# Output projection of a hybrid attention block: seven block products for the pooled channels, three raw buffers for the pages, halves of the residual loaded behind them

## The chip, the cores and the metric

The kernel runs on one core of one Trainium2 chip. The metric is the device time of one execution in microseconds (us). The kernel before took 1030.73 us, the median of 3 runs (1030.71 to 1030.99). The engines are named as the profile names them: PE (TensorE, the matrix unit), DVE (VectorE), ACT (ScalarE), POOL (GpSimd) and SP (SyncE, which issues most of the DMA transfers). Each engine takes its instructions in the order in which the program wrote them, and an instruction that waits holds up everything behind it on its engine.

## The reference

One block over x (1024 tokens of 1024 channels, float32): attention with forget gates on 8 heads of 64, beside it four groups of 128 channels of causal pooling, one output projection over both, and a gated MLP.

```python
h = rmsnorm(x, norm1_g[layer])
proj = jnp.einsum('bsd,de->bse', h, w_in[layer])
...
attn = forgetting_attention(to_heads(q), to_heads(k), to_heads(v), log_f)
attn = attn.transpose(0, 2, 1, 3).reshape(B, S, ATTN_WIDTH)
pool = multiscale_pool(u, w_pool[layer], pool_scale[layer])
mixed = jnp.concatenate([attn, pool], axis=-1)
x = x + jnp.einsum('bse,ed->bsd', mixed, w_out[layer])
h2 = rmsnorm(x, norm2_g[layer])
gate = jnp.einsum('bsd,df->bsf', h2, w_gate[layer])
up = jnp.einsum('bsd,df->bsf', h2, w_up[layer])
x = x + jnp.einsum('bsf,fd->bsd', jax.nn.silu(gate) * up, w_down[layer])
return rmsnorm(x, final_g)
```

The change is in the line `x = x + mixed @ w_out`: 1024 tokens x 1024 channels times 1024 x 1024.

## The kernel before, in words

**Precision.** A float32 operand is kept as two tiles, a high and a low part (`split`, L119: ACT copies the high part, L120; DVE or POOL subtracts it from the source, L121). One product is three matmuls into the same PSUM bank (`mm3`, L159 to L163: high by high, high by low, low by high). In the profile the page of W_out is h_wo, l_wo (hl_wo where both parts lie in one tile), the page of the mixed channels h_mix, l_mix. A page is 128 channels by 1024 (tokens, or output channels): 512 KB raw, one DMA to a tile r_wo or r_mix, one copy on ACT, one subtraction on DVE or POOL.

**Order.** The program runs first the value and pooling projections, then `project(0)` (queries and keys of a pair of heads), and then `attend(0)` to `attend(3)` (L711), one for each pair of heads. The pool results go to DRAM (mixd, pages 4 to 7) before attend 0 begins. `attend` writes the steps of its eight jobs (a head and a block of 256 queries each) one after the other and takes, behind each step, pieces of a generator `fill`, so many for each job as `counts` says. A job's steps are: scores of the next job (z, two matmuls a bank, L617 and L618), on DVE the masked reduction (p<-z,wmask, L620), on ACT the exponential (L626), on DVE the reciprocal (rr, L628), on POOL the normalisation (p<-p,rr, L629), on PE the transposes of p (tp, L643), their copies th on ACT (L647) and tl on DVE (L648), the value products (po, L657), and at, which goes to mixd. Fill is what PE does in between: in attends 0 to 2 the query, key and value products of the pairs to come (qk, hTh and hTl are the normalised input), in attend 3 the output projection. The tiles s_0 and s_1 hold the queries and keys of a head; they are put together by moves from a tile hi and one lo (L569 to L573), and four augmented rows come from augd (L549), all issued on SP.

**Output projection.** Its eight pages of 128 channels are taken in three parts over all 8 row blocks of 128 tokens (the order is `ORDER`, 0, 4, 1, 5, 2, 3, 6, 7) and both halves of the output channels. `first_rows` (L832; banks o4) takes pages 4 and 5, `second_rows` (L859; banks o6) takes 6, 7 and 0, and `last_row` (L888; banks o2), behind attend 3, takes 1, 2 and 3. Each block is summed in a bank of 128 x 512 (tag "m", two of them) and then added on DVE to x2, which begins as the residual x (L814, L826; x_r and x_s in the profile). x2 lies where hTh and hTl lay: it can be loaded only when the last qk matmul of attend 3's queries and keys has read them. `first_chunk` loads and splits page 4 of both operands and loads page 5 of mix during attend 2. All raw pages share the tag "wr" with two buffers, or take what `first_rows` names. `x2_load` (L797) loads a whole row of x, 512 KB.

**SP's queue** carries the pages, the rows of x, the moves into s and the stores of at, in the order of the program. There are no priorities: a load that waits for its buffer holds up what is written behind it.

**Other names.** vpool's tag "vc" holds pf01 (a pooling tile), later values of a pair of heads, page VC, and last t4l of the MLP, which r_gu_P (its first weights, L1011) precedes. `wmask` is the causal mask, wr a raw page, NPAIR is 4, PAIR is (2, 3, 0, 1).

## Time and profile before

| what | us |
|---|---|
| median of the runs | 1030.73 |
| the profiled execution | 1031.67 |
| its span in the trace | 1029.9 |
| VectorE busy | 780.2 |
| ScalarE busy | 473.2 |
| GpSimd busy | 398.2 |

Busy time by stage, from the windows of the trace:

| from to | what runs | PE | DVE | POOL | DMA share |
|---|---|---|---|---|---|
| 90 to 124 | end of the pooling, start of attend 0 | 34.00 of 34 | 15.79 | 2.94 | 0.48 |
| 124 to 260 | attends 0 to 2 | 136.00 of 136 | 91.78 | 33.87 | 0.36 |
| 264 to 282 | start of attend 3 | 17.33 of 18 | 15.95 | 6.73 | 0.91 |
| 282 to 300 | attend 3 | 18.00 of 18 | 14.63 | 6.90 | 0.59 |
| 300 to 351 | attend 3 to its end | 51.00 of 51 | 34.29 | 21.36 | 0.23 |

The granted clock of TensorE is 1.00 in each of these windows. Busy time of PE is counted from a matmul's start to its modelled end, and matmuls overlap; a gap shorter than that overlap doesn't show in it. Waits are put down to what came last.

### The profile page before, as it was taken

What the parts mean: (1) busy time and instruction counts of PE and PEld (TensorE: products, weight loads), DVE (VectorE), ACT (ScalarE), POOL (GpSimd) and SP (SyncE); (2) the same over time, 40 slices, a digit from 0 to 9 for tenths busy, and PEclk for the clock granted to TensorE, in tenths of its full rate; (3) what the DMA queues carried; (4) which work ended last, traced back from release to release, by engine and by line L of the source; (5) the groups of instructions that cost most, each with busy time, mean ns of one, the idle gap of its engine ahead of it and who ended that gap; (6) DMA issues with size and microseconds to landing.
All of it is one profiled execution on the core that took longest, in us unless ns stands there. A gap on an engine that the chain in (4) does not pass through costs nothing.

```text
span 1029.9 us, 15123 instructions
## 1 busy us (share of the span) xinstructions
PE 1020.5 (99%) x5428; PEld 878.3 (85%) x5428; DVE 780.2 (76%) x1232; ACT 473.2 (46%) x759; POOL 398.2 (39%) x317
## 2 busy tenths in 40 slices
PE   9999999999999999999999999999999999999997
PEld 8988888998888888888888888888888888888886
DVE  7565566776786579887978767676777999888887
ACT  7434355665665257544443343343443443333346
POOL 4350121214336043366656646647546610000045
PEclk9999999999999999999999999999999999999999
DMA  7214434333643134333222423333336774353424
GB/s 252 53 46 143 106 81 103 83 95 95 220 176 110 47 118 133 93 113 92 93 82 93 133 83 104 121 104 111 103 121 227 282 251 165 134 187 96 154 93 164
DMA packets 108795, 130.28 MB, mean 126 GB/s; under 512 B 8040, under 2 KB 71024, under 8 KB 108720
## 3 DMA queue, kind: packets, MB, share of 16 engines
q1 hardware_dynamic: 97216, 108.18, 33.5%
q10 hardware_dynamic: 10784, 19.16, 4.9%
q0 software_dynamic: 720, 1.97, 0.5%
q8 instruction: 43, 0.70, 0.3%
q14 instruction: 32, 0.26, 0.1%
HBM read 86.29 MB, written 33.03 MB: 116 GB/s over the span
## 4 chain that ended last, share of the span: by engine, by line
PE 95%; DVE 2%; DMA 1%; issue 1%; ACT 1%; POOL 0%; ACTq 0%; POOLq 0%; DVEq 0%
PE gu_P L162 10%; PE gu_P L161 10%; PE gu_P L163 10%; PE d L161 6%; PE d L163 6%; PE d L162 6%; PE po L657 3%; PE tp L643 3%; PE qk L161 3%; PE qk L162 3%; PE qk L163 3%; PE o L162 3%; PE o L163 3%; PE o L161 3%; PE v L374 2%; PE z L618 2%
## 5 line engine op out<-in xcount | busy, mean ns | idle before, releaser
L162 PE MATMUL d<-d,d 128*128 128x512 f32 (+1 forms) x308 | 118.7, 388 | 0.0
L163 PE MATMUL d<-d,d 128*128 128x512 f32 (+1 forms) x308 | 118.0, 388 | 0.0
L629 POOL TENSOR_SCALAR p<-p,rr 128x128 f32<-128x128 f32 (+3 forms) x64 | 48.8, 769 | 177.1 <-DVE rr L628 135.8
L161 PE MATMUL d<-d,d 128*128 128x512 f32 x308 | 108.0, 388 | 0.0
L120 ACT ACTIVATE d<-r_f 128x1536 fp32r<-128x1536 f32 (+1 forms) x28 | 38.7, 1384 | 107.5 <-PE d L162 103.1
L1579 POOL TENSOR_SCALAR sse<-sse 128x1 f32<-128x1 f32 x7 | 3.5, 494 | 167.6 <-ACT junk L1575 167.6
L162 PEld LDWEIGHTS d<-d,d 128*128 128x128 f32 x308 | 57.8, 188 | 12.1 <-DVE d L121 0.2
L163 PEld LDWEIGHTS d<-d,d 128*128 128x128 f32 x308 | 57.8, 188 | 11.9
L161 PEld LDWEIGHTS d<-d,d 128*128 128x128 f32 x308 | 57.8, 188 | 11.9
L120 ACT ACTIVATE gu_P_h<-s 128x1024 fp32r<-128x1024 f32 (+1 forms) x38 | 36.4, 967 | 61.9 <-PE gu_P L162 31.1
L626 ACT ACTIVATE p<-p,mn 128x128 f32<-128x128 f32 (+3 forms) x64 | 49.4, 773 | 32.0 <-DVE mn L620 29.0
L121 DVE TENSOR_TENSOR gu_P_l<-s,gu_P_h 128x1024 fp32r<-128x1024 f32 (+1 forms) x38 | 54.9, 1454 | 6.6 <-ACT gu_P_h L120 6.4
L648 DVE TENSOR_TENSOR tl<-tp,th 128x512 fp32r<-128x512 f32 (+1 forms) x80 | 49.5, 633 | 9.6 <-ACT th L647 8.5
L121 DVE TENSOR_TENSOR d<-r_f,d 128x1536 fp32r<-128x1536 f32 (+1 forms) x28 | 45.8, 1636 | 6.6 <-ACT d L120 6.5
L163 PE MATMUL qk<-hTh,l_qk 128*128 128x512 f32 x128 | 50.7, 396 | 0.0
L161 PE MATMUL qk<-hTh,h_qk 128*128 128x512 f32 x128 | 50.6, 395 | 0.0
L162 PE MATMUL qk<-hTl,h_qk 128*128 128x512 f32 x128 | 50.4, 394 | 0.0
L1684 DVE TENSOR_TENSOR x2f_s<-d,x2f_s 128x512 f32<-128x512 f32 x64 | 42.4, 683 | 9.9 <-PE d L163 9.9
L647 ACT ACTIVATE th<-tp 128x512 fp32r<-128x512 f32 (+1 forms) x80 | 42.5, 551 | 16.2 <-PE tp L643 13.2
L1161 ACT ACTIVATE sn_sU<-gu_P 128x512 f32<-128x512 f32 x44 | 26.2, 595 | 47.7 <-PE gu_P L163 33.1
L620 DVE CUSTOM_DVE_ANT_0 p<-z,wmask 128x128 f32<-128x128 f32 (+3 forms) x64 | 33.7, 535 | 13.6 <-PE z L618 9.7
L643 PE MATMUL tp<-ident,p 128*128 128x128 f32 x288 | 43.2, 274 | 0.0
(1180 smaller groups left out, 3376.6 us busy)
## 6 DMA issues: line engine op xcount, KB each, us to landing
r_f<-hsdP SPq DMA_DIRECT2D x77, 256.0 KB
r<-in_w_gate_dram SPq DMA_DIRECT2D x44, 256.0 KB
r<-in_w_up_dram SPq DMA_DIRECT2D x44, 256.0 KB
r_wd<-in_w_down_dram SPq DMA_DIRECT2D x22, 512.0 KB
hsdP<-f ACTq DMA_DIRECT2D x40, 256.0 KB
s<-hi SPq DMA_DIRECT2D x64, 128.0 KB
hsdP<-h ACTq DMA_DIRECT2D x23, 256.0 KB
x<-in_x_dram SPq DMA_DIRECT2D x8, 512.0 KB
```

The lines of the kernel that those rows point to most:

```text
L120: mark["hi"] = nc.scalar.activation(out=hi, in_=src, func=AF.Copy)
L121: return eng.tensor_tensor(out=lo, in0=src, in1=f32(hi), op=ALU.subtract)
L161: nc.tensor.matmul(ps, lh, rh, start=start, stop=False, **kw)
L162: nc.tensor.matmul(ps, lh, rl, start=False, stop=False, **kw)
L163: mark["mm"] = nc.tensor.matmul(ps, ll, rh, start=False, stop=stop, **kw)
L620: nc.vector.tensor_tensor_reduce(out=pr[:, n0:n1], in0=z, in1=wmask[:, S - n + n0 : S - n + n1], scale=1.0, scalar=mn, op0=ALU.add, op1=AL ...
L626: nc.scalar.activation(out=pr[:, :n], in_=pr[:, :n], func=AF.Exp, scale=-1.0, bias=mn, accum_out=rs)
L629: nc.gpsimd.tensor_scalar(out=pr[:, :n], in0=pr[:, :n], scalar1=rr, scalar2=1.0, op0=ALU.mult, op1=ALU.mult)
L643: nc.tensor.transpose(tp[:, w : w + P], probs[h, 2 * sb + a][:, s * P : (s + 1) * P], ident)
L647: nc.scalar.activation(out=th[:, :w], in_=tp[:, :w], func=AF.Copy)
L648: nc.vector.tensor_tensor(out=tl[:, :w], in0=tp[:, :w], in1=f32(th[:, :w]), op=ALU.subtract)
L1684: added = nc.vector.tensor_tensor(out=row, in0=ps, in1=row, op=ALU.add)
```

## The change

The pooled channels are pages 4 to 7, 512 of the 1024 in the sum. Tokens are cut into two halves of 512, channels 512 to 1023 into two halves of 256 and output channels into two halves of 512, so that this part is a product of 2 x 2 blocks. Before it took 8 block products; now it takes 7 (P1 to P7), whose operands are blocks or sums of blocks of mix and of W_out. Each block product is 24 matmuls of 128 x 512: four row blocks of 128 tokens, for each two pages of 128 channels, three matmuls each. Page 0 is added to the same banks with `whole`, in part as products of their own (`alone`), and pages 1, 2 and 3 stay in the last rows.

The sums of blocks are formed in attends 0 and 1 by `side_steps`, a second generator: four rounds, two for W_out and two for mix. A round loads four half rows of 128 x 512 quarters (1 MB) into vpool's "vc", makes four sums of 128 x 512 on POOL and stores 1 MB to DRAM (sumd). The pages of P1 to P7 are loaded from mixd, W_out or sumd in halves of 256 KB. Raw pages have two buffers "wr" and a third, "or"; the pages of the last rows ("LATE") come in halves into "hi". A product's bank is read by DVE, added to x2, while the bank stays open and the next product of the chain is added to it. Rows of x are loaded as halves, from the fifth step on behind the page that was issued last.

```diff
+    def quarter_load(r):
+        kind, i = rounds[r]
+        t = quarters[r] = vpool.tile([P, 4, 512], F32, tag="vc", bufs=1, name=f"quarters{r}")
+        for k in range(2):
+            dst = t[:, 2 * k : 2 * k + 2, :].rearrange("p a e -> p (a e)")
+            nc.sync.dma_start(out=dst, in_=page_source(kind, NPAIR + 2 * k + i))
+    def quarter_sums(r):
...
+        for out, in0, in1, op in todo:
+            nc.gpsimd.tensor_tensor(out=out, in0=in0, in1=in1, op=op)
+            yield
+            yield
+    def side_steps():
+        for r in range(len(rounds)):
+            quarter_load(r)
+            for _ in range(3):
+                yield
+            yield from quarter_sums(r)
+            for _ in range(2):
+                yield
+            quarter_store(r)
+            yield
...
-    attend(0, project(1), [5, 4, 4, 3, 8, 6, 6, 0])
-    attend(1, both(project(2), project_v23()), [10, 7, 6, 8, 10, 8, 12, 0])
+    side = side_steps()
+    attend(0, project(1), [5, 4, 4, 3, 8, 6, 6, 0], side=side)
+    attend(1, both(project(2), project_v23(side)), [10, 7, 6, 8, 10, 8, 12, 0], side=side)
...
-    fill = both(first_rows(), second_rows())
+    fill = output_steps()
...
+    def part(ps, k, c, start, stop):
+        (ah, al), (bh, bl) = operands["mix", k], operands["wo", k]
+        for i in range(2):
+            ts, hs = slice(i * 512 + c * P, i * 512 + (c + 1) * P), slice(i * 512, (i + 1) * 512)
+            mm3(ps, ah[:, ts], al[:, ts], bh[:, hs], bl[:, hs], start and i == 0, stop and i == 1, True)
...
+    SPLITS = [
+        ("mix", "P2", M, G, -1), ("wo", "P2", O, V, 0), ("mix", "P7", M, G, 2), ("wo", "P7", O, V, 3),
+        ("mix", "P4", ST1, G, 5), ("wo", "P4", VC, V, 6), ("mix", "P1", M, G, 8), ("wo", "P1", O, V, 9),
+        ("mix", "P6", M, G, 12), ("wo", "P6", O, G, 13), ("mix", "P5", ST0, G, 14), ("wo", "P5", W, V, 15),
+        ("mix", "P3", ST1, G, 16), ("wo", "P3", VC, G, 18), ("wo", 1, O, V, 24), ("mix", 1, M, G, 24),
+        ("wo", 2, O, V, 26), ("mix", 2, M, G, 27), ("wo", 3, W, V, 30),
+    ]
+    HALF_LOADS = {
+        0: [(0, 0), (1, 0)], 1: [(2, 0), (3, 0)], 5: [(4, 0), (5, 0)], 7: [(6, 0), (7, 0)],
+        12: [(0, 1), (1, 1)], 16: [(2, 1), (3, 1)],
+    }
...
+        def alone(c):
+            for tt in (NH + 2 * c, NH + 2 * c + 1):
+                ps = fresh("o0", tt)
+                whole(ps, tt, 1, True, True)
+                add_to(tt, 1, ps)
+        def link(k, down, right, start, stop, more=False):
+            def do(c):
+                ps = fresh(f"o{k}", c) if start else held[c]
+                part(ps, k, c, start, stop and not more)
+                tt = c + down * NH
+                if more:
+                    whole(ps, tt, right, False, stop)
+                add_to(tt, right, ps)
...
+        order = [(alone, 0), (alone, 1)]
+        order += chain(("P2", 0, 0, True, True, True))
+        order += chain(("P7", 1, 1, True, False), ("P4", 1, 0, False, True, True))
+        order += chain(
+            ("P1", 0, 0, True, False), ("P6", 1, 0, False, False), ("P5", 1, 1, False, False),
+            ("P3", 0, 1, False, True, True),
+        )
...
-    attend(3, fill, [3, 3, 4, 4, 4, 4, 3, 2], drain=False)
+    attend(3, fill, [2, 3, 4, 3, 4, 4, 3, 2], drain=False)
```

The list of PE's instructions has 5404 matmuls and transposes after the change, 5428 before. Three places of the lists follow.

POOL at the start of attend 0, behind the four stores to augd. Before, the normalisations of the first head's blocks (p_0, p_1, ...) are next:

```order
L629 TENSOR_SCALAR p_0_1205<-p_0_1205,rr_0_1213 128x128
L629 TENSOR_SCALAR p_1_1216<-p_1_1216,rr_1_1224 128x256
L629 TENSOR_SCALAR p_2_1258<-p_2_1258,rr_2_1266 128x384
L629 TENSOR_SCALAR p_3_1272<-p_3_1272,rr_3_1280 128x512
L629 TENSOR_SCALAR p_4_1310<-p_4_1310,rr_4_1323 128x640
```

Now, at the same place (quarters_1240 is round 1's tile, quarters_1479 round 2's, in the same memory):

```order
L770 TENSOR_TENSOR quarters_1240<-quarters_1240 128x512 x4
L770 TENSOR_TENSOR quarters_1479<-quarters_1479 128x512 x3
L631 TENSOR_SCALAR p_0_1209<-p_0_1209,rr_0_1217 128x128
L631 TENSOR_SCALAR p_1_1220<-p_1_1220,rr_1_1228 128x256
L631 TENSOR_SCALAR p_2_1265<-p_2_1265,rr_2_1273 128x384
L770 TENSOR_TENSOR quarters_1479<-quarters_1479 128x512
L631 TENSOR_SCALAR p_3_1279<-p_3_1279,rr_3_1287 128x512
```

Seven sums, and with them one round's store and the next round's load, have come between the augd stores and the first normalisation.

SP at the start of attend 3 (r_wo, r_mix are pages, x_r and x_s rows of x, s the operands of the scores). Before:

```order
L754 DMA r_wo_3529<-in_w_out_dram 128x1024
L798 DMA x_r_3491<-in_x_dram 128x1024
L569 DMA s_1_3_0_3168<-hi_3_1_3301 64x512
L570 DMA s_1_3_0_3168<-hi_3_1_3301 64x512
L573 DMA s_1_3_0_3170<-lo_3_3167 64x512
L798 DMA x_r_3491<-in_x_dram 128x1024
L754 DMA r_wo_3541<-in_w_out_dram 128x1024
```

Now (r_mixP_3549 is the raw page of P7's mix, r_woP_3546 that of P2's W_out):

```order
L822 DMA r_mixP_3549<-sumd_mix_1205 128x512
L822 DMA r_mixP_3549<-sumd_mix_1206 128x512
L569 DMA s_1_3_0_3205<-hi_3_1_3338 64x512
L570 DMA s_1_3_0_3205<-hi_3_1_3338 64x512
L573 DMA s_1_3_0_3207<-lo_3_3204 64x512
L891 DMA x_r_3528<-in_x_dram 128x512
L891 DMA x_r_3529<-in_x_dram 128x512
L891 DMA x_s_3531<-in_x_dram 128x512
L822 DMA r_woP_3546<-in_w_out_dram 128x512 x2
```

The first row of x has moved behind the moves into s, as halves of several rows, and the first page of W_out behind three of them.

DVE at the start of attend 3, from the first add into x2 to the low part of P2's W_out page (o_4 to o_7 are the banks of `alone`). Before, the page's low part (l_wo, page 5) stands ahead of the first add, as the first of these rows:

```order
L121 TENSOR_TENSOR l_wo_3537<-r_wo_3529,h_wo_3536 128x1024
L648 TENSOR_TENSOR tl_3_3_3110<-tp_3_3_3105,th_3_3_3109 128x384
L648 TENSOR_TENSOR tl_0_0_3137<-tp_0_0_3132,th_0_0_3136 128x384
L620 ISA p_7_3373,mn_7_0_3377<-z_7_0_3374,wmask 128x512
L620 ISA mn_7_0_3377 128x1
L628 RECIPROCAL rr_6_3357<-rs_6_3355 128x1
L826 TENSOR_TENSOR x_r_3491<-o_0_0_3550,x_r_3491 128x512
```

Now, the last twelve of the eighteen rows that begin with the add of o_4:

```order
L670 TENSOR_TENSOR at_3_3160<-po_3_3070,at_3_3160 64x256
L622 ISA p_7_3410,mn_7_512_3419<-z_7_512_3416,wmask,mn_7_0_3414 128x512
L622 ISA mn_7_512_3419 128x1
L622 ISA p_0_3456,mn_0_0_3460<-z_0_0_3457,wmask 128x128
L622 ISA mn_0_0_3460 128x1
L895 TENSOR_TENSOR x_s_3531<-o_6_3623,x_s_3531 128x512
L650 TENSOR_TENSOR tl_1_0_3295<-tp_1_0_3289,th_1_0_3294 128x512
L622 ISA p_1_3480,mn_1_0_3484<-z_1_0_3481,wmask 128x256
L622 ISA mn_1_0_3484 128x1
L650 TENSOR_TENSOR tl_1_1_3325<-tp_1_1_3320,th_1_1_3324 128x384
L895 TENSOR_TENSOR x_s_3533<-o_7_3628,x_s_3533 128x512
L121 TENSOR_TENSOR l_woP_3584<-r_woP_3546,h_woP_3583 128x1024
```

The page's low part now stands behind four adds, each of which needs its half row of x.

More of the change, by code (lines that the diff above doesn't have):

```diff
@@ L578, in project, with project_v23 @@
                 yield
-    def project_v23():
+    def project_v23(side):
+        for _ in side:
+            pass
         vtile(2)
@@ L709, in tile_kernel, with attend @@
     begun = set()
-    def attend(p, fill, counts, drain=True):
+    def attend(p, fill, counts, drain=True, side=iter(())):
         if p == 0:
@@ L742, in both, with page_source @@
             yield from g
-    attend(0, project(1), [5, 4, 4, 3, 8, 6, 6, 0])
-    attend(1, both(project(2), project_v23()), [10, 7, 6, 8, 10, 8, 12, 0])
+    def page_source(kind, c):
+        row = (PAIR[c] if c < NPAIR else c) * P
+        return mixd[c] if kind == "mix" else w_out[0, row : row + P, :]
+    sumd = {(kind, i): dram.tile([P, 4, 512], F32, name=f"sumd_{kind}{i}") for kind in ("mix", "wo") for i in range(2)}
+    rounds = [("wo", 0), ("wo", 1), ("mix", 0), ("mix", 1)]
+    quarters = {}
@@ new lines, in tile_kernel, with ahead_of @@
+    FIRST_LATE = len(SPLITS) - len(LATE)
+    THIRD.update(entry[:2] for entry in SPLITS[2:FIRST_LATE:3])
+    HALF_LOADS = {
+        0: [(0, 0), (1, 0)], 1: [(2, 0), (3, 0)], 5: [(4, 0), (5, 0)], 7: [(6, 0), (7, 0)],
+        12: [(0, 1), (1, 1)], 16: [(2, 1), (3, 1)],
+    }
+    def ahead_of(s):
+        for n, (kind, c, to, eng, at) in enumerate(SPLITS):
+            if at == s:
+                split_page(kind, c, to, eng)
+                after = n + 1 if (kind, c) in LATE else n + 3
+                if after < len(SPLITS) and (SPLITS[after][:2] not in LATE or (kind, c) in LATE or after == FIRST_LATE):
+                    raw_page(*SPLITS[after][:2])
+        for tt, hf in HALF_LOADS.get(s, []):
+            with tc.issue_after(loads["page"].ins) if s >= 5 else ExitStack():
+                half_load(tt, hf)
@@ L871, in page @@
+    raw_page(*SPLITS[1][:2])
+    raw_page(*SPLITS[2][:2])
+    for tt in range(NH, NT):
+        half_load(tt, 1)
+    ahead_of(-1)
+    fill = output_steps()
+    attend(3, fill, [2, 3, 4, 3, 4, 4, 3, 2], drain=False)
+    last = {
+        k: [operands[kind, 1]] for k, kind in (("lhs", "mix"), ("rhs", "wo"))
+    }
     def page(tag, name):
```

127 lines of the change are left out of this document (72 added, 55 removed).

## The prediction

> **What bounds the kernel now.** I read the page's busy times first, then the chain that ended last, then TensorE's waits, and only then the timeline.
>
> ```profile
> PE 1020.5 (99%) x5428; PEld 878.3 (85%) x5428; DVE 780.2 (76%) x1232; ACT 473.2 (46%) x759; POOL 398.2 (39%) x317
> PE 95%; DVE 2%; DMA 1%; issue 1%; ACT 1%; POOL 0%; ACTq 0%; POOLq 0%; DVEq 0%
> PE o L161 <- ACT h_wo L120: 0.4, 1, 0.4
> PE o L162 <- DVE l_wo L121: 0.2, 1, 0.2
> ```
>
> TensorE (PE) is busy 99% of the span, 95% of the chain lies on it, and in the output projection it waits twice, for one page. So a matmul that goes away is worth its place in PE's queue, and everything else is worth only what it makes PE wait. The price of a matmul is not the mean that the groups give (first row; then the timeline, start and duration):
>
> ```profile
> L162 PE MATMUL o<-l_wo,h_mix 128*128 128x512 f32 x64 | 25.1, 392 | 0.2 <-DVE l_wo L121 0.2
> ...
> 274.22 0.39 PE L163 MATMUL o<-h_wo,hl_mix 128*128 128x512 f32 x1
> 274.44 0.39 PE L161 MATMUL o<-h_wo,h_mix 128*128 128x512 f32 x1
> 274.67 0.39 PE L162 MATMUL o<-l_wo,h_mix 128*128 128x512 f32 x1
> 274.90 0.39 PE L163 MATMUL o<-h_wo,l_mix 128*128 128x512 f32 x1
> ```
>
> One lasts 0.39 us from start to end, but the next starts after 0.22 or 0.23 us: three spacings make 0.68 us, so I price it at 0.2275 us. The 392 ns counts the overlap twice.
>
> **What goes.** Channels 512 to 1023 of the product took 8 blocks x 24 matmuls; now they take 7 x 24. So 24 matmuls go, which is the whole difference in PE's row count: 24 x 0.2275 = 5.46 us (by 392 ns it would be 9.4). The adds of banks into x2 stay 32. The two waits above go as well, because after wo0 the first products now need no second page:
>
> ```profile
> 269.34 0.39 PE L618 MATMUL z<-s,s 68*128 68x512 f32 x1
> 270.16 0.73 PE L161 MATMUL o<-h_wo,h_mix 128*128 128x512 f32 x2 [0.43 <-ACT h_wo L120]
> 270.90 0.27 PE L618 MATMUL z<-s,s 68*128 68x128 f32 x1
> 271.42 0.50 PE L162 MATMUL o<-l_wo,h_mix 128*128 128x512 f32 x1 [0.24 <-DVE l_wo L121]
> ```
>
> The matmul at 269.34 would be followed at 269.57, but the next starts at 270.16, 0.59 late; the narrow one at 270.90 takes about 0.06 and the next is 0.46 late. Together 1.05 us.
>
> **What comes: the sums in attend 0.** VectorE (DVE) reads pf01 last at 93.58 + 1.23 = 94.81, and its space takes the first quarters; SP reaches that load behind the augd rows, at 95.27 + 0.76 = 96.0. The rows are from the timeline (start, duration), a group (busy, mean ns) and the rates of the DMA view.
>
> ```profile
> 93.58 1.23 DVE L121 TENSOR_TENSOR pl<-pf,ph 128x1024 fp32r<-128x1024 f32 x1
> 95.27 0.76 SPq L549 DMA_DIRECT2D s<-augd  x2
> 115.32 1.50 POOL L629 TENSOR_SCALAR p<-p,rr 128x128 f32<-128x128 f32 x3 [38.94 <-DVE rr L628]
> 119.45 0.27 PE L643 MATMUL tp<-ident,p 128*128 128x128 f32 x1
> L121 POOL TENSOR_TENSOR l_u<-r_u,h_u 128x1024 fp32r<-128x1024 f32 x4 | 10.5, 2628 | 10.7 <-ACT h_u L120 10.7
> 350.93 0.33 SPq L880 DMA_DIRECT2D r_mix<-mixd  x1
> 353.44 0.63 ACT L120 ACTIVATE mix_h<-r_mix 128x512 fp32r<-128x512 f32 x1 [2.13 <-DMA r_mix<-mixd]
> GB/s 0 0 0 0 173 15 0 129 70 269 398 386 386 339 293 222 369 345 351 234 234 164 269 316 328 398 316 316 386 398 398 410 445 433 386 386 445 410 375 375
> ```
>
> The last row is the rate from 262 to 276 us, when transfers queue; I take 350 GB/s. A lone 256 KB took 2.51 us to its reader, so about 1.75 beside its bytes. One megabyte is then 1.75 + 3.0 = 4.75 us. A sum over 128x512 is half an l_u: 1.31. The line: load lands 101.3 (0.55 more for the mixd stores beside it), four sums to 106.5, store out by 112.0 (0.75 for the key moves beside it), next load by 117.1, three sums to 121.0. Only then does POOL reach p_0, p_1, p_2, which take 1.5: done at 122.5. Before, POOL was free from 76 us, and p_0 lay ready 3.6 us ahead of its transpose at 119.45. In the new order PE's transpose of p_0 falls 1.36 us later (six more matmuls of 0.2275 ahead of it), that of p_2 at about 121.6. So PE waits 0.9; I take **1.0**, bounds 0 (no neighbours in the queues) and 3.5 (both round trips lose 1.3 to the moves). The later rounds stand ahead of normalisations that are 4 us or more early, and I cost them at nothing; without that cover each is worth up to one sum, 1.3.
>
> The Trainium skill (DMA: Bandwidth & Descriptors, Anatomy of one DMA) has about 2.0 us fixed and 436 GB/s for a transfer from GpSimd's queue, hence an estimate of 4.4 us for a megabyte, and this wait would shrink to nothing and the total to 1027.1. The 5.42 us for half a megabyte below speaks against such a rate in a crowded queue.
>
> **What comes: the entry of attend 3.** The first x rows now arrive as halves behind pages, and four adds follow single products. Below, a row of the chain that ended last, then the timeline and the groups of 260 to 351 us.
>
> ```profile
> 263.61 5.42 DMA r_wo<-in_w_out_dram
> 263.64 0.33 PE L617 MATMUL z<-s,s 128*128 128x384 f32 x1
> 264.51 0.48 SPq L569 DMA_DIRECT2D s<-hi  x1
> 266.33 1.54 SPq L798 DMA_DIRECT2D x_r<-in_x_dram  x1
> L814 DVE TENSOR_TENSOR x_r<-o,x_r 128x512 f32<-128x512 f32 x14 | 9.5, 683 | 4.6 <-PE o L163 4.5
> L648 DVE TENSOR_TENSOR tl<-tp,th 128x512 fp32r<-128x512 f32 x20 | 13.5, 686 | 2.8 <-ACT th L647 2.6
> L648 DVE TENSOR_TENSOR tl<-tp,th 128x384 fp32r<-128x384 f32 x13 | 7.1, 551 | 0.3
> L620 DVE CUSTOM_DVE_ANT_0 p<-z,wmask 128x512 f32<-128x512 f32 x5 | 3.4, 682 | 0.6 <-PE z L618 0.6
> L668 DVE TENSOR_TENSOR at<-po,at 64x256 f32<-64x256 f32 x13 | 5.5, 420 | 4.4 <-ACT at L667 4.3
> 270.14 1.23 DVE L121 TENSOR_TENSOR l_wo<-r_wo,h_wo 128x1024 fp32r<-128x1024 f32 x1 [1.31 <-ACT h_wo L120]
> ```
>
> PE's rows from the first z behind the last qk product (263.64) to the first that reads the low part of woP2: 14 matmuls of 0.2275, 22 z (3.87), 21 transposes (2.34), 20 value products (2.14), together 11.5 us, so it is wanted at 275.2. On SP the halves stand behind three s moves, where a row went out at 266.33; with 1.75 and a quarter to three quarters of a megabyte at 350 the first lands at about 269.2. DVE is in order: behind the first add stand three more adds, tl of 128x384, 128x512 and 128x384, two reductions of z 7, the small ones of z_0 and z_1, at, and then l_woP2. By starts (each about 0.07 before the end of the one ahead): 2.5 + 1.6 + 2.1 + 0.5 + 1.2 = 7.9, done at 277.1. PE waits **1.9**. Bounds: 0.9 (half lands a microsecond earlier) and 4.5 (it lands as late after its issue as the page in the chain's row, 5.42 us). Queued behind are the reductions and tl of the next heads, which hold z banks; that is in the upper bound.
>
> **What comes: behind it.** Two more groups of DVE from 260 to 351 us carry this part.
>
> ```profile
> L620 DVE CUSTOM_DVE_ANT_0 p<-z,wmask 128x384 f32<-128x384 f32 x5 | 2.7, 548 | 0.4 <-PE z L618 0.4
> L121 DVE TENSOR_TENSOR hl_wo<-r_wo,hl_wo 128x1024 fp32r<-128x1024 f32 x1 | 1.2, 1216 | 0.0
> ```
>
> hl_woP4 (low part) stands on DVE directly behind the reduction of z_2 and is wanted 1.7 us after that z's last matmul; 0.55 + 1.22 + 0.1 is 1.9: **0.3** with ACT's part, bounds 0 and 2. Banks are now read open: P1, P6, P5, P3 share one, and the next product may not write before DVE has added it. At two places only the other bank's six matmuls lie between, 6 x 0.2275 = 1.36 us; an add takes 0.68, which leaves as much for the hand-over. That hides unless the wo1 and wo2 splits (1.22 + 2 x 0.69 = 2.6) stand ahead of the add, as they do once: **0.3**, bounds 0 and 1.0. Last, r_gu_P's first DMA waits for PE's last use of woP3 and stands on SP ahead of wo3's second half:
>
> ```profile
> 354.16 0.69 DVE L121 TENSOR_TENSOR mix_l<-r_mix,mix_h 128x512 fp32r<-128x512 f32 x1 [0.41 <-ACT mix_h L120]
> 264.00:282.00 18.00, 17.33 (x101) 15.02 (x101) 15.95 (x41) 13.40 (x27) 6.73 (x5) 1.00 0.91 300
> ```
>
> A half took from 350.93 to 354.85, 3.9 us, to be split; with 0.45 for the row ahead 4.4. Its low part is wanted 4.3 us after that use: **0.4** with the gate's bytes beside it, bounds 0 and 1.2. The extra splits (ten rows on ACT, five on DVE) run where DVE is 15.95 of 18 us busy, which is why I trust no cover at the entry. From the last rows on, all five queues have the same rows in the same order, so what PE has won there it keeps.
>
> **Sum.** Profiled execution 1031.67 (span 1029.9 and 1.77 around it): - 5.46 - 1.05 + 1.0 + 1.9 + 0.3 + 0.3 + 0.4 = 1029.06. It was 0.94 above the median of the runs, 1030.73, so 1028.1 there.
>
> **Rivals.** (1) All covers hold: the stalls come to 0 to 2 us, the time to 1024.2 to 1026.2. For it: the bound of zero is real for four of five terms. Against: DVE's load at the entry. (2) The entry's burst lands late and every later DVE row with it: stalls of 5.5 to 8.6, 1029.7 to 1032.8, no change that can be told. For it: DMA is 0.91 busy from 264 to 282. (3) Slower: POOL's line in attend 0 takes over. If the megabyte legs run at the rate at which the key moves go (about 200 GB/s, next row), each is 7.0 us, sums end at 126.2, p_2 at 127.7, 6.1 us after PE wants it; sums at 1.87 (what such an operation takes on POOL when DVE reads beside it) add 3.9. With 2.9 from the other terms: 1033.2 to 1037.1.
>
> ```profile
> GB/s 351 337 2 19 117 201 201 117 0 239 361 0 152 215 199 33 325 274 0 152 213 199 101 0 0 0 155 215 199 31 0 0 75 213 192 119 0 0 0 0
> L1197 POOL TENSOR_TENSOR f<-sn_sP,sn_sU 128x512 f32<-128x512 f32 x8 | 15.0, 1870 | 0.0
> ```
>
> That row is 90 to 125 us: 200 in the moves, gaps between them, which a megabyte over all partitions may fill. It turns slower than before when the three legs take more than 18.5 us together; I have 15.8.
>
> **The numbers.** Forecast (stalls 2 to 5.5: 1026.2 to 1029.7) 0.45; rival 1 0.22; rival 2 0.18; rival 3 0.15. A measurement of this kernel tells about 0.2%, 2.06 us, from no change: faster is below 1028.67, slower above 1032.79. Faster: 0.22 and two thirds of the forecast's, 0.52; same: the rest of it and nearly all of rival 2, 0.32; slower: 0.16. The range leaves out a tenth at each end: 1024.6 to 1033.4.
>
> **What would show it.** 5404 matmuls and transposes on PE; a PE gap at the transposes of p_0 to p_2 near 121 us whose releaser is POOL; a gap before the first product with l_woP2 with DVE's adds ahead of it; no wait for h_wo at 269. I am wrong if PE waits somewhere not named here, above all for a normalisation behind rounds 2 to 4, or if the two traces drift apart after 410 us.

## The result, and the profile after

The changed kernel takes 1039.46 us (median of 4 runs, 1037.67 to 1040.88), the kernel before beside it 1030.86 (1030.71 to 1031.46): ratio 1.0081, 95% interval 1.0064 to 1.0099. It is slower by 8.6 us. 1028.1 was forecast, and the time lies above the range. The profiled execution of the changed kernel takes 1039.72 us, 8.05 more than the profiled one of before (1031.67).

The page of the changed kernel, busy times and the engines of the chain that ended last:

```profile
PE 1022.0 (98%) x5404; PEld 875.5 (84%) x5404; DVE 784.0 (76%) x1237; ACT 479.0 (46%) x768; POOL 425.2 (41%) x337
PE 89%; DMA 3%; DVE 3%; issue 1%; ACT 1%; POOL 1%; SPq 0%; ACTq 0%; POOLq 0%; DVEq 0%
```

The 24 matmuls are gone (5404 against 5428), yet PE is busy longer, 1022.0 against 1020.5 us: the same matmuls last longer somewhere. And the chain has left PE: 95% of it lay there, now 89%, with DMA and DVE at 3% each.

PE's waits over the changed kernel's whole span (what waits, what released it: us in total, times, longest):

```profile
PE o L161 <- ACT h_wo L120: 2.0, 2, 1.7
PE oP L161 <- ACT h_woP L120: 1.8, 1, 1.8
...
PE qk L161 <- ACT p L628: 0.9, 1, 0.9
PE tp L645 <- DVE tl L650: 0.8, 1, 0.8
PE po L659 <- DVE tl L650: 0.5, 1, 0.5
```

These make 6 us, less than half of the 13.5 (8.05, and the 5.46 of the matmuls) that have to be found. The windows show where PE had less to do; the columns are length, then busy time and instructions of PE, PEld, DVE, ACT and POOL, PE's granted clock, DMA share and GB/s. Before:

```profile
282.00:300.00 18.00, 18.00 (x115) 16.10 (x114) 14.63 (x40) 9.59 (x18) 6.90 (x8) 1.00 0.59 220
300.00:318.00 18.00, 18.00 (x108) 15.75 (x107) 14.83 (x38) 13.96 (x28) 11.37 (x10) 1.00 0.38 120
351.00:375.00 24.00, 24.00 (x116) 20.02 (x114) 12.89 (x19) 8.37 (x14) 4.18 (x7) 1.00 0.32 112
```

After:

```profile
264.00:282.00 18.00, 16.18 (x90) 13.23 (x89) 13.83 (x38) 12.26 (x24) 7.36 (x5) 0.95 0.73 213
282.00:300.00 18.00, 17.75 (x97) 15.37 (x95) 11.71 (x28) 10.26 (x19) 9.69 (x9) 0.96 0.82 272
300.00:318.00 18.00, 16.34 (x90) 13.34 (x91) 14.48 (x39) 10.40 (x23) 6.51 (x7) 1.00 0.45 139
351.00:375.00 24.00, 21.45 (x99) 16.67 (x98) 15.15 (x23) 10.81 (x18) 8.12 (x6) 1.00 0.39 122
```

PE is short of work at three places of attend 3: the entry (264 to 282), the middle (300 to 318) and the end (351 to 375). In the first two rows its clock is 0.95 and 0.96 where it was 1.00; that is where the matmuls grew longer.

To add the losses up I gave each row of PE, in order, the spacing it has when nothing disturbs it (0.2275 us for 128x512, as in the prediction, and so for the narrower ones) and subtracted the running sum from the start times. What that difference grows by in a stage was lost there, by waits or by the clock. Minus the same of before, each from one profiled execution, in us (good to about half a microsecond, since a loss at a border can fall to either side); the last column is the time until 420 us at half clock, of which at most half is lost:

```
                           to 262   262-290   290-312   312-374   sum   at half
changed kernel               2.1       3.5       3.7       3.9    13.2       3.4
before, 24 matmuls less      0.0       0.2      -0.1       1.5     1.6       0.0
changed, no sums             0.0       3.9       4.3       4.7    12.9       3.4
changed, wo3 raw apart       1.4       4.3       1.0       4.7    11.4       3.4
changed, five buffers        2.0       5.2       4.7       4.6    16.5      10.2
changed, sums contiguous     1.4       2.7       7.3       5.1    16.5      13.7
changed, x rows whole        2.9       4.5       3.3       4.1    14.8       3.4
changed, all rows whole      3.2       3.4       0.8       6.0    13.4       6.8
changed, woP2 first          1.5       3.8       3.6       3.7    12.6       3.4
changed, 9 more at entry     2.3       0.3       7.2       3.4    13.2       6.8
changed, 18 more at end      2.5       4.6       3.2       0.7    11.0       3.4
five buffers, x ahead        2.4       3.7       0.8       3.5    10.4       3.4
no x rows                    1.4       0.9       3.5       4.7    10.5       3.4
five buffers, no x rows      1.3       0.1       2.3       2.7     6.4       0.0
before, loads in halves     -0.1       4.2       0.8       0.2     5.1       3.4
```

For the changed kernel 13.2 - 5.46 = 7.7 of the 8.05 us. The rows below it are the experiments; matmuls that they add count as work and not as lost.

Entry, after, from the timeline: SP issues woP2's load, ACT makes its high part, PE reads it.

```profile
270.89 0.86 SPq L822 DMA_DIRECT2D r_woP<-in_w_out_dram  x2
277.60 1.06 ACT L120 ACTIVATE h_woP<-r_woP 128x1024 fp32r<-128x1024 f32 x1 [2.53 <-DMA r_woP<-in_w_out_dram]
278.71 0.51 PE L161 MATMUL oP<-h_woP,h_mixP 128*128 128x512 f32 x1 [1.77 <-ACT h_woP L120]
281.91 0.63 PE L161 MATMUL oP<-h_woP,h_mixP 128*128 128x512 f32 x1
282.33 0.63 PE L162 MATMUL oP<-l_woP,h_mixP 128*128 128x512 f32 x1
283.84 0.39 PE L163 MATMUL oP<-h_wo,hl_mix 128*128 128x512 f32 x1
```

The page takes 6.7 us from its issue to its first reader. PE waits 1.77 us, and then matmuls start 0.42 us apart, not 0.2275. Two-microsecond windows show why:

```profile
278.00:280.00 2.00, 1.29 (x9) 1.21 (x10) 0.99 (x2) 2.00 (x5) 0.00 (x0) 1.00 0.58 153
280.00:282.00 2.00, 2.00 (x8) 1.31 (x7) 2.00 (x7) 1.95 (x7) 0.00 (x0) 0.55 0.85 260
282.00:284.00 2.00, 2.00 (x7) 1.58 (x6) 1.91 (x6) 1.47 (x5) 1.84 (x3) 0.60 0.85 264
284.00:286.00 2.00, 2.00 (x11) 1.62 (x10) 0.86 (x4) 0.00 (x0) 1.36 (x3) 1.00 0.71 221
```

Behind the wait the clock is at half: a mean of 0.55 over 2 us is 1.8 us at half, 0.60 is 1.6. These 3.4 us do the work of 1.7, so 1.7 us more are lost. DVE's adds, which the prediction had ahead of the page's low part, come second:

```profile
279.01 0.69 DVE L895 TENSOR_TENSOR x_s<-o,x_s 128x512 f32<-128x512 f32 x1 [1.08 <-DMA x_s<-in_x_dram]
279.62 1.22 DVE L121 TENSOR_TENSOR l_woP<-r_woP,h_woP 128x1024 fp32r<-128x1024 f32 x1
```

The low part is done at 280.84, and the first product that reads it starts at 280.89, about 0.3 us later than it could at half clock.

Middle, after: the chain that ended last, 292 to 307 us.

```profile
290.04 2.42 POOL l_mixP L121
...
292.85 4.24 DMA r_woP<-in_w_out_dram
...
297.18 1.07 ACT h_woP L120
...
298.27 1.24 DVE l_woP L121
...
299.52 0.32 SPq L822
...
299.89 3.77 DMA r_mixP<-sumd_mix
...
303.74 0.04 ACT h_mixP L120
...
304.70 0.48 ACT th L649
...
305.21 0.04 DVE tl L650
```

No matmul stands in it. A page's low part on POOL frees a raw buffer, the next page goes into it, ACT makes its high part, DVE its low part, that frees the buffer, and the next page is issued. From one load (292.46) to the next (299.52) it is 7.0 us, with three buffers 2.3 us a page. And ACT is in order: th, the high half of the transposed weights of attention, waits behind h_mixP, tl behind th, PE behind tl. Which page's high part stands ahead of th is a matter of ACT's order; in this execution it is h_mixP, which waits 1.93 us for its page, and hl_woP, whose load went out earlier (297.49) and for which ACT doesn't wait, comes after it:

```profile
303.74 1.06 ACT L120 ACTIVATE h_mixP<-r_mixP 128x1024 fp32r<-128x1024 f32 x1 [1.93 <-DMA r_mixP<-sumd_mix]
306.62 1.06 ACT L120 ACTIVATE hl_woP<-r_woP 128x1024 fp32r<-128x1024 f32 x1
```

End, after, timeline:

```profile
361.47 0.33 SPq L996 DMA_DIRECT2D r_mix<-mixd  x1
362.65 0.33 SPq L822 DMA_DIRECT2D r_wo<-in_w_out_dram  x1
366.05 0.63 ACT L120 ACTIVATE h_wo<-r_wo 128x512 fp32r<-128x512 f32 x1 [1.45 <-DMA r_wo<-in_w_out_dram]
366.73 0.50 PE L161 MATMUL o<-h_wo,mix_h 128*128 128x512 f32 x1 [1.72 <-ACT h_wo L120]
```

wo3's halves are issued behind the last splits, and PE has come to them before they land.

### The profile page after: what moved, and what is told of

Read it like the earlier page. It is cut to its first block, busy times and chain, and to the rows that moved or that the text cites. A ratio compares the mean times of both kernels' runs of the same rounds, so it can differ in the third digit from the quotient of the medians.

```text
span 1037.9 us, 15214 instructions
## 1 busy us (share of the span) xinstructions
PE 1022.0 (98%) x5404; PEld 875.5 (84%) x5404; DVE 784.0 (76%) x1237; ACT 479.0 (46%) x768; POOL 425.2 (41%) x337
## 4 chain that ended last, share of the span: by engine, by line
PE 89%; DMA 3%; DVE 3%; issue 1%; ACT 1%; POOL 1%; SPq 0%; ACTq 0%; POOLq 0%; DVEq 0%
PE gu_P L162 10%; PE gu_P L161 10%; PE gu_P L163 10%; PE d L162 6%; PE d L161 6%; PE d L163 6%; PE qk L161 3%; PE qk L163 3%; PE qk L162 3%; PE po L659 3%; PE tp L645 3%; PE v L374 2%; PE u L162 1%; PE u L161 1%; PE u L163 1%
## 5 line engine op out<-in xcount | busy, mean ns | idle before, releaser
L163 PEld LDWEIGHTS d<-d,d 128*128 128x128 f32 x308 | 57.8, 188 | 11.8
```

The costliest lines, as they stand in the source:

```text
L163: mark["mm"] = nc.tensor.matmul(ps, ll, rh, start=False, stop=stop, **kw)
```

## The experiments

Ratios are to the kernel before, in five rounds beside it, with 95% intervals; losses by stage are in the table above.

**What are 24 matmuls worth, and do the sums cost anything?** The kernel before without page 0 for four of its row blocks, and the changed kernel with plain quarters in place of the sums:

```diff
-            yield from rows2(second["mix"], second["wo"], tt, "o6")
+            n = 2 if tt in ORDER[:4] else 3
+            yield from rows2(second["mix"][:n], second["wo"][:n], tt, "o6")
```

> The kernel before, with 24 matmuls left out and nothing else: page 0 of both operands is left out for four of the eight row blocks in the second part of the projection (the sum lacks it there). If a matmul is worth its spacing, 0.2275 us, everywhere in this stage, the time falls by 5.5 us, to 1025.4. If DVE or the pages set the pace of attend 3, so that the gain of fewer products was never there, it falls by less than 3 us.

```diff
-    side = side_steps()
+    side = iter(())
...
-                src = sumd[kind, i][:, QUARTER[kind][c], :]
+                q = QUARTER[kind][c]
+                src = page_source(kind, NPAIR + q // 2 * 2 + i)[:, q % 2 * 512 : (q % 2 + 1) * 512]
```

> The changed kernel without the sums of blocks: no loads of quarters, no sums on POOL, no stores in attends 0 and 1, and the pages of sums are loaded from plain quarters of mix and W_out (so the products are of other operands). Alignment of the two traces puts 2.1 us of the loss between 90 and 257 us, 3.6 at the entry of attend 3, 3.6 between 288 and 312, 4.0 at the end of attend 3. If the loss before 257 comes from the sums, that 2.1 goes: 1037.4. If the sums and their traffic were the whole cause, the time falls below 1030. If it was the other order of the instructions, nothing changes: 1039.5.

24 matmuls less alone: 1028.06 us against 1031.33, ratio 0.9969 (0.9959 to 0.998). Of 5.46 us, 3.3 arrive; 1.5 are lost between 340 and 350 us, 0.6 of them in waits for th and tl of the last heads, which fewer products now cover. Without the sums: 1039.53 us, 1.0085 (1.0071 to 1.0098), no gain. The loss in attend 0 to 2 is gone, and attend 3 gives all of it back. The sums don't set the time.

**Is it wo3, or the number of buffers?** wo3's raw halves in a tile of their own, loaded with mix2; and five raw buffers in place of three (the pages of the last rows then come whole and pass through them too):

```diff
-            ts = [ap_.tile([P, 512], F32, tag="hi", bufs=2, name=f"r_{kind}{c}_{i}") for i in range(2)]
+            pl, tag = (op, "lr") if (kind, c) == ("wo", 3) else (ap_, "hi")
+            ts = [pl.tile([P, 512], F32, tag=tag, bufs=2, name=f"r_{kind}{c}_{i}") for i in range(2)]
...
```

> The changed kernel, where the raw halves of wo3 have buffers of their own and are loaded ahead of those of mix2, rather than into the two buffers that wo2 and mix2 pass through. The trace of the changed kernel waits 1.72 + 0.26 + 0.22 us at the end of attend 3 for wo3's parts. If the buffers are the cause, some 3.5 to 4 us go: 1035.7. If SP's queue (the rows ahead) or the split on ACT is the cause, under 1 us goes.

```diff
-            where, tag, bufs = (op, "or", 1) if (kind, c) in THIRD else (wpool, "wr", 2)
+            where, tag, bufs = (op, "or", 3) if (kind, c) in THIRD else (wpool, "wr", 2)
...
-                after = n + 1 if (kind, c) in LATE else n + 3
+                for after in {0: [4], 1: [5, 6]}.get(n, [n + 5]):
...
```

> The changed kernel with five raw buffers for the pages in place of three (two more in memory that lies idle in attend 3), the last pages among them, and each page loaded when the one five before it is split. If PE waits because a page's load must wait for the split of the page three before it, the losses at the entry, in the middle and at the end go: 3.6 + 3.6 + 4.0 = 11 us, to about 1028.5. If the loss is DVE's and ACT's order (adds, splits and reductions in one queue), or the adds that wait for the halves of x, it stays above 1034.

wo3 apart: 1039.37 us, 1.008 (1.0067 to 1.0094). PE no longer waits for wo3's landing, but 1.77 us (until 364.79) for an add that stands on DVE behind wo3's low parts (361.02, 3.11 us), and 2.6 us for woP2 at the entry. The middle falls to 1.0, though its pages have three buffers as before: ACT now has hl_woP (303.04) ahead of h_mixP (305.51) and waits for no page. Five buffers: 1046.85 us, 1.0156 (1.0142 to 1.0171), worse: the x rows, which go out behind pages, now go out behind two pages more, and DVE waits 2.64 us for one (until 289.22). At the end PE waits 2.42 us (until 365.75) for an add, but this one stands on DVE behind two low parts of pages (360.01, 4.50 us). About 3 us more are lost behind 374, outside the table.

**Is it the short rows?** Halves of a page or of x have 2 KB a partition. The DMA view from 270 to 278 us, first before, then after:

```profile
DMA packets 821, 2.96 MB, mean 370 GB/s; under 512 B 90, under 2 KB 90, under 8 KB 820
```

```profile
DMA packets 1219, 2.13 MB, mean 266 GB/s; under 512 B 168, under 2 KB 202, under 8 KB 1219
```

Half as many packets again carry less. So: the kernel before with its x rows and these pages as halves; and the changed kernel with the sums side by side in DRAM (one load a page), with whole rows of x at the places of the first halves, and with both and the mixd pages whole as well.

```diff
-        nc.sync.dma_start(out=t, in_=mixd[c] if kind == "mix" else w_out[0, row : row + P, :])
+        page = mixd[c] if kind == "mix" else w_out[0, row : row + P, :]
+        for i in range(2):
+            hs = slice(i * 512, (i + 1) * 512)
+            nc.sync.dma_start(out=t[:, hs], in_=page[:, hs])
...
```

> The kernel before, with the rows of x and the pages of attends 2 and 3 loaded as two halves of 256 KB (2 KB to a partition) in place of one transfer of 512 KB (4 KB to a partition); nothing else changes. From 270 to 278 us the kernel before moved 2.96 MB in 820 packets with the engines full, the changed one 2.13 MB in 1219 packets at 0.92. If the short rows are what makes the changed kernel's pages late, the halves slow this kernel at the entry of attend 3 too: by 2 to 5 us, 1033 to 1036. If they only show lateness that comes from elsewhere (raw buffers, order), it stays at 1030 to 1031.5.

```diff
...
+            src = sumd[kind][:, QUARTER[kind][c], :, :].rearrange("p a e -> p (a e)")
+            loads["page"] = nc.sync.dma_start(out=whole, in_=src)
...
```

> The changed kernel, with the two halves of a page of sums side by side in DRAM: one transfer of 4 KB a partition in place of two of 2 KB for 8 of the 14 pages. If the row length counts, pages land earlier and the time falls by 2 to 4 us, to about 1036. If the buffers or the order set the pace, under 1 us.

```diff
-        nc.sync.dma_start(out=x2_half(tt, hf), in_=xf[tt * P : (tt + 1) * P, hf * 512 : (hf + 1) * 512])
+        nc.sync.dma_start(out=x2[tt], in_=xf[tt * P : (tt + 1) * P, :])
...
```

> The changed kernel, with whole rows of x (512 KB, 4 KB a partition) loaded where the first halves are, and none of the later halves. By the row length: the transfers of 264 to 312 us take less time in all (2 MB more at the entry, 2 MB less behind it), the entry loses up to 2 us and the middle and the end win 2 to 4: 1037 to 1039. If it is the bytes at the entry that count, the entry loses 3 us or more and the time rises above 1041.

```diff
-                    nc.sync.dma_start(out=mixd[NPAIR + g, :, ts], in_=mo)
+                    nc.sync.dma_start(out=mixq[g // 2, tb, :, g % 2, :], in_=mo)
...
```

> The changed kernel with whole rows of x, sums side by side and the pooled pages of mix side by side by quarters, so that only three pages of W_out are still loaded in halves. By the row length most of the losses of attend 3 go: 1029 to 1034. If the raw buffers (three) set the pace, it stays above 1037.

Halves cost the kernel before 6 us: 1037.57, 1.0054 (1.0041 to 1.0068), most of it at the entry. They are shorter rows and also twice as many transfers; which of the two costs was not separated. But whole rows gain the changed kernel nothing that can be told: 1043.38 us, 1.0114 (1.0099 to 1.0129), with the sums contiguous; 1041.48, 1.0099 (1.0085 to 1.0113), with whole x rows; 1038.26, 1.0069 (1.0055 to 1.0083), with all of it. The first is slower than the changed kernel, against both expectations; its trace has 10.2 us at half clock in a row from 301.82 and 3.4 more from 370.08, where the changed kernel has 3.4 in all. Halves are dear, yet they aren't alone what holds this kernel.

**Fill the gaps.** Nine matmuls more (page 0 once more, into the bank that the next product overwrites) ahead of the first product with woP2; and 18 more (page 1) ahead of the last rows:

```diff
+                for _ in range(3 if (k, c) == ("P2", 0) else 0):
+                    whole(ps, NH, 0, True, True)
                 part(ps, k, c, start, stop and not more)
```

> The changed kernel with nine matmuls more (page 0 once more into the bank that the first block product then overwrites) right ahead of the first product with woP2, where TensorE waits 1.8 us and then runs at half clock for 3.4 us. Theory (the idle gap is what lowers the clock, and the landing of woP2 sets the end of the gap): the nine matmuls, 9 x 0.2275 = 2.05 us, stand in the gap; 0.3 us more work than gap, 1.7 us of half clock less: 1.4 us below the changed kernel, about 1038.0, with no slow stretch behind 280 us. Rival (the clock falls for another reason, the transfers or VectorE's load): the slow stretch stays, 0.3 us above, about 1039.8.

```diff
+    ps = bank("again", "m", 2)
+    for _ in range(6):
+        mm3(ps, ah[:, 0:P], al[:, 0:P], bh[:, 0:512], bl[:, 0:512], True, True)
```

> The changed kernel with 18 matmuls more (a product with page 1 repeated into a bank of its own) ahead of the last rows, where TensorE waits for wo3. Theory (the last pages land at a time that attend 3 and its transfers set, not TensorE's place in its queue, so a shorter projection only waits longer there): 18 x 0.2275 = 4.1 us of work stand in 2.2 to 3.2 us of waits: 0.9 to 1.9 us above the changed kernel, 1040.3 to 1041.4. Rival (the waits at the end move along with TensorE): the whole 4.1 us, about 1043.5.

At the entry the fill does what was expected (loss there 0.3, clock 1.00 from 278 to 284), but the time is 1043.85 us, 1.012 (1.0106 to 1.0134). What was won is lost in the middle, and more. The timeline of that run:

```profile
295.83 1.06 ACT L120 ACTIVATE h_mixP<-r_mixP 128x1024 fp32r<-128x1024 f32 x1 [2.76 <-DMA r_mixP<-mixd]
297.29 1.06 ACT L120 ACTIVATE h_woP<-r_woP 128x1024 fp32r<-128x1024 f32 x1 [0.41 <-DMA r_woP<-in_w_out_dram]
298.26 0.92 ACT L628 ACTIVATE p<-p,mn 128x768 f32<-128x768 f32 x1
298.38 2.04 DVE L121 TENSOR_TENSOR l_woP<-r_woP,h_woP 128x1024 fp32r<-128x1024 f32 x1 [3.48 <-ACT h_woP L120]
301.01 0.39 PE L659 MATMUL po<-th,v 128*128 128x256 f32 x1 [2.79 <-DVE at L670]
```

ACT and DVE stop for P1's pages with attention's p, at and tl queued behind them, PE has 2.79 us of nothing, and two stretches of 3.4 us at half clock follow, from 301.51 and from 308.34. Both of my expectations missed this. At the end the theory holds: 18 matmuls, 4.1 us, move the time to 1040.78 us, 1.0093 (1.008 to 1.0107), 1.3 above the changed kernel; the wait for wo3 is gone:

```profile
367.56 0.63 ACT L120 ACTIVATE h_wo<-r_wo 128x512 fp32r<-128x512 f32 x1 [1.80 <-DMA r_wo<-in_w_out_dram]
370.05 0.39 PE L161 MATMUL o<-h_wo,mix_h 128*128 128x512 f32 x1
```

In the changed kernel the start of the last rows is set by when wo3 lands and not by PE's work ahead of it. (In this execution wo3 came 1.5 us later than in the changed kernel's, 367.56 against 366.05, and 1.1 us more were lost at the entry.)

**Earlier woP2.** The third raw buffer for woP2, woP7 and so on, so that its load waits for no buffer:

```diff
-    THIRD.update(entry[:2] for entry in SPLITS[2:FIRST_LATE:3])
+    THIRD.update(entry[:2] for entry in SPLITS[1:FIRST_LATE:3])
```

> The changed kernel with the third raw buffer given to woP2, woP7 and so on in place of mixP7 and so on, so that woP2's load waits for no buffer at the entry of attend 3 and goes out ahead of the x rows. Theory (what is lost at the entry comes from the late issue of woP2, 270.9 us): woP2 lands some 3 us earlier, the wait of 1.8 us and the slow stretch behind it go: 2.5 to 3.5 us below the changed kernel, 1036 to 1037. Rival (the entry is bound by the bytes of x rows and pages together, whatever their order): the wait moves to an add for x, no change, 1038.5 to 1040.5.

woP2 is there 8 us earlier (h_woP at 269.57), and the time stays: 1039.84 us, 1.0083 (1.007 to 1.0097). The loss at the entry stays, 3.8 against 3.5: PE now waits twice for an add of x, 1.05 us until 285.85 and 1.02 until 289.67, which is the rival on record. The middle has 3.6 against 3.7, with the stretch at half clock now there, from 303.87.

**Buffers and x rows apart and together.** Five buffers with each step's x rows ahead of its pages; three without the x rows; five without them (the residual is left out in these two):

```diff
...
-        for tt, hf in HALF_LOADS.get(s, []):
-            with tc.issue_after(loads["page"].ins) if s >= 5 else ExitStack():
-                half_load(tt, hf)
+        for tt, hf in HALF_LOADS.get(s, []):
+            half_load(tt, hf)
         for n, (kind, c, to, eng, at) in enumerate(SPLITS):
...
```

> The changed kernel with five raw buffers for the pages (the two more in free space), and the x rows of each step issued ahead of the step's pages, not behind them. Theory (the ring of three raw buffers sets the pace from 285 to 312 us: a page is loaded, split into its high and low part, and only then is the next one issued): the loss at 300 to 312 us goes, 3 to 4 us below the changed kernel, 1035 to 1036.5. Rival (the bytes of pages and x rows together set it): no change, 1038.5 to 1041, the loss only elsewhere.

```diff
-        nc.sync.dma_start(out=x2_half(tt, hf), in_=xf[tt * P : (tt + 1) * P, hf * 512 : (hf + 1) * 512])
+        fresh_rows.add((tt, hf))
...
-        nc.vector.tensor_tensor(out=out, in0=ps, in1=out, op=ALU.add)
+        first = (tt, hf) in fresh_rows
+        fresh_rows.discard((tt, hf))
+        nc.vector.tensor_tensor(out=out, in0=ps, in1=f32(operands["mix", 0][0][:, 0:512]) if first else out, op=ALU.add)
```

> The changed kernel without the loads of the x rows (the residual is left out: the first add into each half row takes a page that lies there in place of x), 4 MB less, the same instructions on TensorE and VectorE. Theory (ring of three buffers): the loss at the entry, 3.6 us, goes, because adds no longer wait for x and woP2 lands earlier, the one at 300 to 312 us stays: 1035 to 1036. Rival (bytes): both go, 1031 to 1033.

> Both: five raw buffers and no loads of x rows (the residual left out as in the run beside it). Theory (ring, and the entry's x rows): both losses go, what stays is attend 0 to 2 and the end, 1031 to 1033. If it stays above 1036, neither buffers nor bytes set the pace, but the order of splits on ScalarE, VectorE and GpSimd.

By stage these three fit the theory: five buffers take the middle from 3.7 to 0.8, no x rows take the entry from 3.5 to 0.9 and leave the middle at 3.5, both leave 0.1 and 2.3. But that the ring of three buffers makes the loss in the middle isn't shown: five buffers alone leave 4.7 there, and with three it falls to 1.0 (wo3 raw apart) and 0.8 (all rows whole). By time the theory holds far less: 1040.11 us, 1.008 (1.0067 to 1.0092); 1037.55, 1.0064 (1.0051 to 1.0077); 1036.58, 1.0052 (1.0038 to 1.0066). The traced execution of the first is its fastest, 1037.79, so its row is better than its median. Each time a good part comes back behind: with five buffers DVE's low part of a last page takes 2.58 us (GpSimd makes another one beside it) and stands ahead of at, and PE waits 2.06 us at 354; without x rows it waits 2.10 us for wo3, then half clock. Even with neither limit the kernel stays above before, and above 1036, where the expectation puts it down to the order of the splits on ACT, DVE and GpSimd. In that trace, as in that of five buffers alone, two low parts of pages hold DVE, here from 349.96 to 354.46, and PE waits 2.42 us, until 355.70, for an add into x2 behind them; no run changes that order by itself.

**Is it the gap that halves the clock?** wo5's low part by GpSimd in the kernel before, made once and made twice, was to make PE wait:

```diff
-        rhs.append(split_page("wo", 5, O, nc.vector))
+        rhs.append(split_page("wo", 5, O, nc.gpsimd))
```

> The kernel before with the low part of one page (wo5) made by GpSimd in place of VectorE, so that TensorE stops once, near 271 us, for about 1.6 us. Theory (a gap of one to two microseconds is enough to lower the clock for 3.4 us): the gap and 1.7 us behind it: 3.0 us above before, about 1034.2, with one slow stretch behind 271 us. Rival (the clock doesn't follow so short a gap): 1.3 us above, about 1032.5, clock as before.

```diff
+        raw5 = raw_pages["wo", 5]
...
+        nc.gpsimd.tensor_tensor(out=rhs[1][1], in0=raw5, in1=f32(rhs[1][0]), op=ALU.subtract)
```

> The kernel before with the low part of one page (wo5) made by GpSimd, and made twice over (the same result), so that TensorE waits for GpSimd near 271.5 us, 2 to 3 us long. Theory (a gap of about two microseconds lowers the clock to half for 3.4 us): the gap and 1.7 us more: 1034.5 to 1036, with a slow stretch behind the gap. Rival (the clock doesn't follow so short a gap): the gap alone, 1032.5 to 1034, clock as before.

Neither tells anything: 1031.07 us, 1.0003 (0.9994 to 1.0012), and 1032.36, 1.0008 (0.9999 to 1.0017). The order of instructions is planned when the kernel is built, and in neither trace does PE wait for that low part. So it was measured by itself, in 25 bursts of matmuls with a chain on VectorE between them:

```diff
+            for _ in range(count):
+                nc.tensor.matmul(bank, left, right, start=True, stop=True)
...
+            nc.vector.tensor_tensor(out=hold, in0=bank, in1=rows[1][:, 0:512], op=ALU.add)
+            for k in range(gap - 1):
+                nc.vector.tensor_tensor(out=hold, in0=hold, in1=rows[1][:, 0:512], op=ALU.subtract)
...
```

> A small program in place of the kernel (it only stores rows of x, one half row of them added to a product): 25 bursts of 48 to 64 matmuls of 128x512, 11 to 15 us each, and between them gaps in which TensorE waits for 1, 2, 3, 4, 6 or 8 additions of 128x512 on VectorE and one short operation, about 1.0, 1.6, 2.2, 2.8, 4.1 and 5.3 us, each gap four times. Theory (a gap of one to two microseconds can halve the clock for 3.4 us, by where it falls): some of the gaps of 1 to 3 us are followed by a burst with a stretch at half clock, others not; those over 4 us always. Rival (short gaps don't, and the slow stretches of the changed kernel have another cause): no slow stretch behind gaps under 3 us.

Its timeline and windows of 1 us, at one gap of 1.91 us:

```profile
31.93 1.68 PE L43 MATMUL bank<-right,left 128*128 128x512 f32 x4 [1.91 <-DVE left L49]
```

```profile
32.00:33.00 1.00, 1.00 (x4) 0.76 (x5) 0.00 (x0) 0.00 (x0) 0.00 (x0) 0.71 0.00 0
33.00:34.00 1.00, 1.00 (x4) 0.81 (x3) 0.00 (x0) 0.00 (x0) 0.00 (x0) 0.50 0.00 0
34.00:35.00 1.00, 1.00 (x4) 0.81 (x3) 0.00 (x0) 0.00 (x0) 0.00 (x0) 0.50 0.00 0
35.00:36.00 1.00, 1.00 (x4) 0.76 (x4) 0.00 (x0) 0.00 (x0) 0.00 (x0) 0.59 0.00 0
36.00:37.00 1.00, 1.00 (x6) 0.83 (x5) 0.00 (x0) 0.00 (x0) 0.00 (x0) 1.00 0.00 0
```

3.4 us at half clock with neither DMA nor another engine at work. Counted over all gaps: 1.11 us, 0 of 4 followed by a slow stretch; 1.84 to 1.91 us, 1 of 4; 2.56 us, 2 of 4; 3.3 us, 2 of 4; 4.74 and 6.2 us, all 8. So a gap is enough by itself, in these counts from somewhere between 1.1 and 1.9 us on. Where it falls decides: the slow stretches of this program start at times that lie whole multiples of 3.413 us apart, and when time is cut at these points, every piece at full clock in which PE stood idle for 2.0 us or more was followed by half clock, none with 1.75 or less, and one of the two with 1.9. The changed kernel's wait of 1.77 us and its slow stretch are of this kind, though the limit is less sharp in the kernels, where half clock followed pieces with as little as 1.2 us idle. Its 1.72 us at 366 had none; 1.2 of them fell into one piece.

## Why the prediction was wrong

- **24 x 0.2275 = 5.46** was right as work and wrong as time. Alone they give 3.3 us. The step that failed is the sentence that a matmul that goes away is worth its place in PE's queue: attend 3's last heads and wo3 come at times of their own, and with less work ahead of them PE stands and waits. 18 matmuls put ahead of wo3 cost 1.3 of their 4.1 us. The two waits at 269 went as forecast (1.05 in the sum; PE has won 0.8 by 272), and so, in the changed kernel, held the sentence that PE keeps from the last rows on what it has: behind 374 another 0.4 us are lost.
- **The entry, 1.9 in the sum (bounds 0.9 to 4.5).** A gap was there ahead of the first product with woP2, as forecast, but it was ended by ACT's high part of a page that had landed late, not by DVE's adds; that it lasted 1.77 us, near the forecast's 1.9, is luck. The sum has no line for the landing of that page. Against before 3.5 us were lost, where the prediction has 1.9 less the two waits saved, 0.85. The sum took 350 GB/s for halves; the traffic ran at 266 from 270 to 278 us. The first halves of x went out at 269.29, where it has 266.33; 2.1 of these 3.0 us had been lost before 262. And it had no price for the clock: 1.7 of the 3.5. What would have been needed was the DMA rate in the new mix of rows, and a line for woP2 itself, whose load stands behind three x halves in the list of SP.
- **Behind it, 0.3 + 0.3.** 3.7 were lost. hl_woP4 and open banks are not what failed; no term was there for three raw buffers with 7.0 us from load to load, and none for a page's high part that stands on ACT ahead of attention's th and p while it waits for DMA. Whether the buffers or the order on ACT and DVE counts for more, the runs leave open. That is the largest omission. Rival 2 came nearest (every later DVE row late with the entry, 8.6 us at most, chance 0.18), but the middle doesn't follow from the entry: with the entry's loss at 0.3 or 0.9 it still lost 7.2 or 3.5.
- **wo3's second half, 0.4 (0 to 1.2).** 3.9 were lost at the end, nearly all of it between 354 and 372; the 1.5 that the 24 matmuls less cost alone stand earlier, before 350. That r_gu_P stands ahead of the second half was right and small. What the term left out is the first half: the two were issued at 362.65 and 363.90, behind the last splits, and PE waited 1.72 us for the first. With buffers of their own the end loses 4.7 all the same: the page is there, but its low parts hold DVE.
- **The sums in attend 0, 1.0.** Nearly right. POOL's rows of the changed kernel:

```profile
118.06 2.66 POOL L770 TENSOR_TENSOR quarters<-quarters 128x512 f32<-128x512 f32 x2 [1.42 <-DMA quarters<-in_w_out_dram]
120.70 1.39 POOL L631 TENSOR_SCALAR p<-p,rr 128x128 f32<-128x128 f32 x3
```

The sums end at 120.7 (forecast 121.0), p_2 at 122.1 (122.5), and about 0.5 us are lost. A part of this is luck: the load landed at 118.06 and not at 117.1, but one of the three sums had already run on its first half. That later rounds cost nothing was wrong: in attend 1 PE loses 1.5 us more, mostly at one product qk at 167.09 (0.88 us of wait, put down to ACT's p; DVE's last read of a qk bank ends at 166.94). It goes when the sums are left out; whether by POOL's time or because the planner then orders the transposes differently was not separated. But none of it matters while attend 3 gives it back. By the figure of the Trainium skill that the prediction weighed (DMA: Bandwidth & Descriptors, Anatomy of one DMA) PE would not have waited for p_2, and the trace is against that: the store of round 1 and the load of round 2 took 11.8 us together (106.28 to 118.06), not twice 4.4.
- **Rival 3** had the sign right and the place wrong: 1033.2 to 1037.1 from POOL in attend 0, where leaving the sums out altogether gains nothing.

What the runs don't settle is what holds the kernel with both limits gone, and so how the loss splits between buffers, bytes and the order of the splits: with five buffers and no x rows, 6.4 us of losses remain up to 374 us, and 1.8 more by 390. The waits named there are nearly all for DVE, the longest 2.42 us for an add of x2. Each of these runs also has an order of its own from the planner, and a single profiled execution, in which one stretch at half clock more or less is 1.7 us.

## What to carry to other kernels

A matmul that is taken away is worth its time only where nothing else arrives by the clock behind it: put work back into the waits and see whether the time moves, before counting it. Where a page is needed soon after the one before it, reckon the ring: load, high part, low part, over the number of buffers, and look at what stands behind each split on an in-order engine. A fix at one wait of such a ring says little until the next one has been looked at: here the repair of a single wait mostly moved the loss, and none brought back the time of before.
